# Experts in the order of their place in the group, result rows kept by expert number, and the final sums and norm beside the last experts

## The chip, the cores and the metric

The kernel runs on one core of one Trainium2 chip. The metric is the device time of one execution in microseconds, the median of three runs. The profiles come from single executions, recorded by the chip's profiler. TensorE multiplies matrices into PSUM, VectorE and ScalarE work on elements, GpSimd computes some elements and issues the indirect DMAs (gathers and scatters of rows by an index), and SyncE issues all other DMAs. Each engine, and each queue of DMA issues, executes its own list strictly in order.

## The reference

One layer of an encoder on 1024 tokens of width 1024 (batch 1, float32): a mixer of two attentions with a residual, a mixture of experts with a residual, and a last RMS norm. The mixer is not touched here. What matters:

```python
h = rms_norm(x, g_moe)
# 4 groups of 8 experts: the best group g_idx of each token, then the best 2 of its 8 experts
expert_ids = g_idx * 8 + idx                  # both experts of a token lie in one group
weights    = g_w * vals / sum(vals)
y_e        = (silu(h @ w1[e]) * (h @ w3[e])) @ w2[e]    # 1024 -> 512 -> 1024, 32 experts
x          = x + sum over the token's two experts of weight * y_e
out        = x * rsqrt(mean(x*x) + eps) * g_final
```

## The kernel before

**Stages.** Projections, attentions, the mixer's output with the routing of each tile of 128 tokens (`route_tile`), then the experts (`stage_moe`), then the final sums and norm. The values after the mixer (`x2`) and their norm (`h2`) are written to DRAM; the last four of the eight tiles of `x2` also stay in SBUF (`fx`).

**Routing and slots.** Each expert has 96 slots (`CAP`). A one-hot matmul over all tiles leaves in PSUM, for each expert and slot, the row of the result and the weight. `slots` makes from it three tiles with a column for each expert: `gi`, the token to gather; `yi`, the row of the result to write; `wt`, the weight. The result lies in a DRAM buffer `ys` of 2048 rows: row t for the token's best expert, row 1024 + t for its second. `ys` has been cleared to zeros before. Indices of empty slots are out of bounds, and the indirect DMA leaves them out. Tokens beyond the 96 go through `overflow`, a conditional part at the end that is skipped in these runs.

**One expert.** For expert e the weights w1, w3 and w2 come in six pieces of 1 MB (`expert_piece`, two for each matrix). Each is split into a rounded part (ScalarE, L45) and a remainder (VectorE, L46) in halves of 128x1024, and each product takes three matmuls (L1007 to L1009, L1039 to L1041). The 96 rows of `h2` are gathered (GpSimd) and transposed (TensorE); after w1 and w3 the gate's product (VectorE, L1018) waits for TensorE; the products are transposed and go through w2; ScalarE evicts with the weight, and GpSimd scatters the rows to `ys`. While expert e does this, w1 of expert e + 1 is multiplied, the rows of e + 2 are transposed and those of e + 3 gathered.

**Slots of the weights.** There are eleven buffers of 128x2048 (1 MB). `slot()` takes the first of a list and puts it back at its end, so the pieces go round; `slot(True)` takes one out of the round for good. A new tile in a buffer waits until all uses of the tile before it are done:

```python
    def slot(self, keep=False):
        p, i = self.free.pop(0)
        if not keep:
            self.free.append((p, i))
        return p.tile([128, 2 * D], F32, name=f"mraw{i}")
```

A piece is also issued only when the piece three before it has landed. All weight pieces, and the loads of the tail, stand in SyncE's one queue.

**Order.** TensorE's order is the written one (`manual_schedule`). For the other engines and queues a planner chooses: in its own model of the times it takes, whenever an engine is free, the ready instruction that is written first. The order is then fixed, and on the chip each instruction waits for its inputs in its place. `issue_after` adds an order between two instructions of one engine.

**The tail.** At expert 31 `final_rows` loads the gains and the four tiles of `x2` that are not in SBUF (L1192, L1198), and `final_sums` loads for each tile the rows of both halves of `ys` (L1208, 1 MB). GpSimd adds the first half (L1209). The rows of expert 31 are never written to `ys`: VectorE makes one-hot matrices of its tokens (L1107), and for each tile and 512 columns TensorE adds the second half (by an identity matmul, L1134) and expert 31's rows (two one-hot matmuls, L1135 and L1136), and VectorE adds that to the tile (L1137). The gains are broadcast by TensorE (L1184). `final_norm` takes squares and a square root on ScalarE (L1217, L1219), a reciprocal and the product on VectorE (L1220, L1221) and stores the tile (L1222).

## Time and profile before

| what | value |
|---|---|
| median of three runs | 1570.59 us (1570.49 to 1572.16) |
| the profiled execution | 1570.37 us, of which the profile's span is 1568.6 us |
| busy in the span | TensorE 95%, its weight loads 74%, VectorE 67%, ScalarE 56%, GpSimd 18% |
| chain that ended last | TensorE 81%, VectorE 6%, DMA 5%, ScalarE 2%, issue 3% |
| moved by DMA | 394.94 MB, 252 GB/s on the mean |

The experts run from about 906 us (first gather) to 1526 us, the tail from there to 1568.6. A timeline row gives start, length, engine (SPq is SyncE's DMA queue), line, operation, output<-input, shapes and count; in brackets stands how long the engine was idle before it and what released it. Several equal instructions in a row are merged, with their count behind an x and their common length. `mhi` and `mlo` are the rounded part and the remainder of a weight, `mraw` a buffer of the round, `m` and `mpy` PSUM tiles of the products, `mg` the gate's product.

### The profile page before, as it was taken

What the parts mean: (1) busy time and instruction counts of PE and PEld (TensorE: products, weight loads), DVE (VectorE), ACT (ScalarE), POOL (GpSimd) and SP (SyncE); (2) the same over time, 40 slices, a digit from 0 to 9 for tenths busy, and PEclk for the clock granted to TensorE, in tenths of its full rate; (3) what the DMA queues carried; (4) which work ended last, traced back from release to release, by engine and by line L of the source; (5) the groups of instructions that cost most, each with busy time, mean ns of one, the idle gap of its engine ahead of it and who ended that gap; (6) DMA issues with size and microseconds to landing.
All of it is one profiled execution on the core that took longest, in us unless ns stands there. A gap on an engine that the chain in (4) does not pass through costs nothing.

```text
span 1568.6 us, 21877 instructions
## 1 busy us (share of the span) xinstructions
PE 1483.5 (95%) x7713; PEld 1167.3 (74%) x7713; DVE 1050.8 (67%) x1926; ACT 881.6 (56%) x1328; POOL 289.4 (18%) x279
## 2 busy tenths in 40 slices
PE   7999999999999999989999869999999999999996
PEld 6998888788888888877888746666667666666663
DVE  6212566666655555628474579989998888888866
ACT  5312455455555555424121268878888777777763
POOL 2302122222212222200200211041001111111023
PEclk9999999999999999999999979999999999999998
DMA  8327888776545454389637579999999999999845
GB/s 268 123 95 211 232 239 239 222 219 181 160 136 174 135 155 128 106 252 284 228 122 288 207 242 372 368 359 370 381 380 378 366 350 346 353 347 350 316 173 216
DMA packets 179236, 394.94 MB, mean 252 GB/s; under 512 B 21714, under 2 KB 99538, under 8 KB 154546
## 3 DMA queue, kind: packets, MB, share of 16 engines
q1 hardware_dynamic: 172066, 376.89, 70.9%
q0 software_dynamic: 7056, 16.62, 3.3%
q8 instruction: 61, 1.00, 0.3%
q14 instruction: 53, 0.43, 0.1%
HBM read 324.36 MB, written 77.25 MB: 256 GB/s over the span
## 4 chain that ended last, share of the span: by engine, by line
PE 81%; DVE 6%; DMA 5%; issue 3%; ACT 2%; SPq 1%; POOL 0%; DVEq 0%; ACTq 0%; POOLq 0%
PE pz L308 7%; PE pz L310 7%; PE pz L309 7%; PE m L1008 6%; PE m L1009 6%; PE m L1007 6%; PE mpy L1041 3%; PE mpy L1039 3%; PE mpy L1040 3%; PE pt L389 3%; DMA mraw<-in_w_dram 3%; DVE mlo L46 3%; PE po L475 3%; PE ps L363 2%; PE ps L364 2%
## 5 line engine op out<-in xcount | busy, mean ns | idle before, releaser
L46 DVE TENSOR_TENSOR mlo<-mraw,mhi 128x1024 fp32r<-128x1024 f32 x384 | 450.1, 1220 | 41.3 <-ACT mhi L45 39.5
L45 ACT ACTIVATE mhi<-mraw 128x1024 fp32r<-128x1024 f32 x384 | 391.7, 1056 | 65.1 <-PE m L1009 47.7
L1008 PE MATMUL m<-mlo,XT 128*96 128x512 f32 x512 | 205.2, 401 | 22.4 <-DVE mlo L46 22.4
L308 PE MATMUL pz<-ht,zhi 128*128 128x512 f32 x512 | 214.1, 418 | 0.0
L1007 PE MATMUL m<-mhi,XT 128*96 128x512 f32 x512 | 206.2, 403 | 0.0
L1009 PE MATMUL m<-mhi,XT 128*96 128x512 f32 x512 | 204.8, 400 | 0.0
L310 PE MATMUL pz<-ht,zlo 128*128 128x512 f32 x512 | 201.4, 393 | 0.0
L309 PE MATMUL pz<-ht,zhi 128*128 128x512 f32 x512 | 200.1, 391 | 0.0
L372 ACT ACTIVATE te<-te,nm 128x256 f32<-128x256 f32 (+7 forms) x128 | 99.2, 775 | 118.0 <-DVE nm L368 117.7
L1008 PEld LDWEIGHTS m<-mlo,XT 128*96 128x96 f32 x512 | 84.2, 164 | 64.9 <-DVE mlo L46 31.1
L368 DVE CUSTOM_DVE_ANT_0 te<-ps,nF 128x512 f32<-128x512 f32 (+3 forms) x128 | 74.9, 587 | 61.3 <-PE ps L364 41.6
L310 PEld LDWEIGHTS pz<-ht,zlo 128*128 128x128 f32 x512 | 96.0, 188 | 21.6
L1009 PEld LDWEIGHTS m<-mhi,XT 128*96 128x96 f32 x512 | 83.9, 164 | 35.4 <-issue 0.8
L1007 PEld LDWEIGHTS m<-mhi,XT 128*96 128x96 f32 x512 | 84.0, 164 | 34.3 <-issue 0.5
L308 PEld LDWEIGHTS pz<-ht,zhi 128*128 128x128 f32 x512 | 97.5, 191 | 13.3
L309 PEld LDWEIGHTS pz<-ht,zhi 128*128 128x128 f32 x512 | 96.8, 189 | 13.3
L46 DVE TENSOR_TENSOR PT<-pt,PT 128x512 fp32r<-128x512 f32 (+1 forms) x144 | 76.7, 553 | 44.0 <-ACT PT L45 41.3
L1041 PE MATMUL mpy<-mhi,GT 128*96 128x512 f32 x256 | 101.7, 397 | 2.8 <-DVE GT L46 2.5
L1039 PE MATMUL mpy<-mhi,GT 128*96 128x512 f32 x256 | 102.3, 400 | 0.6 <-ACT GT L45 0.6
L280 POOL TENSOR_TENSOR zlo<-zraw,zhi 128x1024 fp32r<-128x1024 f32 x32 | 77.1, 2411 | 137.5 <-ACT zhi L279 123.4
L1040 PE MATMUL mpy<-mlo,GT 128*96 128x512 f32 x256 | 100.4, 392 | 0.0
L985 POOL DMA_INDIRECT X<-h,sg x32 | 39.2, 1226 | 327.3 <-PE mpt L995 320.3
(263 smaller groups left out, 2821.4 us busy)
## 6 DMA issues: line engine op xcount, KB each, us to landing
mraw<-in_w_dram SPq DMA_DIRECT2D x192, 1024.0 KB, 8.1
zraw<-in_w_in_dram SPq DMA_DIRECT2D x32, 512.0 KB, 4.9
ys<-ylast SPq DMA_DIRECT2D x16, 512.0 KB, 5.3
gscr<-sh SPq DMA_DIRECT2D x32, 256.0 KB, 2.1
o<-oscr SPq DMA_DIRECT2D x8, 1024.0 KB, 8.7
g<-gscr SPq DMA_DIRECT2D x32, 256.0 KB, 4.0
mraw<-ys SPq DMA_DIRECT2D x8, 1024.0 KB, 8.9
xt<-in_x_dram SPq DMA_DIRECT2D x8, 512.0 KB, 6.1
```

Of the source, the lines that this page charges most:

```text
L45: nc.scalar.activation(hi, src, AF.Copy)
L46: nc.vector.tensor_tensor(lo, src, f32(hi), op=OP.subtract)
L308: nc.tensor.matmul(ps, hi[:, k], self.hT[0][:, k, tk], start=(k == 0), stop=False)
L309: nc.tensor.matmul(ps, hi[:, k], self.hT[1][:, k, tk], start=False, stop=False)
L310: nc.tensor.matmul(ps, lo[:, k], self.hT[0][:, k, tk], start=False, stop=(k == KC - 1))
L372: nc.scalar.activation(t[:, :n], t[:, :n], AF.Exp, scale=-1.0, bias=nm, accum_out=rs)
L1007: nc.tensor.matmul(ps, XT[0][:, k], hi, start=(k == 0), stop=False)
L1008: nc.tensor.matmul(ps, XT[0][:, k], lo, start=False, stop=False)
L1009: nc.tensor.matmul(ps, XT[1][:, k], hi, start=False, stop=(k == KC - 1))
L1039: nc.tensor.matmul(ps[n], GT[0][:, k], hi[:, nn], start=(k == 0), stop=False)
L1040: nc.tensor.matmul(ps[n], GT[0][:, k], lo[:, nn], start=False, stop=False)
L1041: self.last_down = nc.tensor.matmul(ps[n], GT[1][:, k], hi[:, nn], start=False, stop=(k == 3))
```

## The change

- The experts are taken by `ORDER`: 0, 8, 16, 24, 1, 9, ..., 31, that is by their place in the group, and for equal places by group. Weights, `gi`, `yi` and `wt` are read by it.
- `route_tile` gives each token's two rows of `ys` by expert number: row t for the lower of its two experts, 1024 + t for the higher (three VectorE instructions more for each tile). So the first half of `ys` is complete when the first 28 experts in the new order are done, and a row of the last expert is always one of the second half.
- Before expert 28 is computed (that is, behind the weight loads of expert 29 in SyncE's queue): the gains (now broadcast by the DMA, 512 KB), the four tiles of `x2`, and the first half of `ys` in four loads of 1 MB through the round. VectorE adds it to the tiles at the end of experts 28 (tiles 0 to 3) and 29 (tiles 4 to 7).
- At expert 29: `x2` and the first half of `ys` are gathered for the last expert's tokens into a buffer of their own (`sl`) and added by VectorE. The down product of the last expert is evicted by VectorE with the weight, onto these rows.
- At the last expert: the second half of `ys`, four loads of 1 MB. VectorE adds it, then each tile is normed and stored. The square root is a power -0.5 on GpSimd (`rstd`).
- The rows of the last expert are normed apart and scattered to the output by token, over the rows that the tiles' stores have written there.
- The one-hot matrices, the sums on TensorE and GpSimd, the broadcast of the gains by TensorE and `tokf` go.

"Expert 28" here and below is the one at place 28 of the order, counted from 0.

```diff
+ORDER = [g * PER_GRP + l for l in range(PER_GRP) for g in range(N_GRP)]
...
-    def rstd(self, pool, ss, n, tag):
-        nc = self.nc
-        m = pool.tile([128, 1], F32, name=tag + "m")
+    def rstd(self, pool, ss, n, tag, q=128):
+        nc = self.nc
+        m = pool.tile([q, 1], F32, name=tag + "m")
         nc.vector.tensor_scalar(m, ss, 1.0 / n, EPS, op0=OP.mult, op1=OP.add)
-        r = pool.tile([128, 1], F32, name=tag + "r")
-        self.pow = nc.gpsimd.tensor_tensor(r, m, self.mhalf[:, 0:1], op=OP.pow)
+        r = pool.tile([q, 1], F32, name=tag + "r")
+        self.pow = nc.gpsimd.tensor_tensor(r, m, self.mhalf[:q, 0:1], op=OP.pow)
         return r
...
-        for k in range(2):
-            nc.vector.tensor_scalar(self.rec[:, :, k, 0], self.tok2[:, :, k], -PAD_ID, None, op0=OP.add)
+        nc.vector.tensor_scalar(self.tok2, self.tok2, -PAD_ID, None, op0=OP.add)
...
+        sw = p.tile([128, 1], F32, name="sw")
+        nc.vector.tensor_scalar(sw, ix[0], ix[1], float(S), op0=OP.is_lt, op1=OP.mult)
+        nc.vector.tensor_add(self.rec[:, t, 0, 0:1], self.tok2[:, t, 0:1], sw)
+        nc.vector.tensor_sub(self.rec[:, t, 1, 0:1], self.tok2[:, t, 1:2], sw)
...
-        nc.vector.tensor_copy(self.wt, tb[:, :, 1])
-        self.tokf = p.tile([CAP, 1], F32, name="stk")
-        self.slots_done = nc.vector.scalar_tensor_tensor(self.tokf, tb[:, N_EXP - 1, 0:1], PAD_ID, fi[:, N_EXP - 1:], op0=OP.add, op1=OP.add)
+        self.slots_done = nc.vector.tensor_copy(self.wt, tb[:, :, 1])
...
-        src = self.a[("w1", "w3", "w2")[wi]][0, e].rearrange("(p c) n -> p c n", p=128)
+        src = self.a[("w1", "w3", "w2")[wi]][0, ORDER[e] if isinstance(e, int) else e].rearrange("(p c) n -> p c n", p=128)
...
-            if hl:
-                split(nc, hl[0][:CAP, nn], hl[1][:CAP, nn], ps[n], wt)
-            nc.scalar.activation(y[:, nn], ps[n], AF.Copy, scale=wt)
+            if xs is not None:
+                nc.vector.scalar_tensor_tensor(xs[:, nn], ps[n], wt, xs[:, nn], op0=OP.mult, op1=OP.add)
+            else:
+                nc.scalar.activation(y[:, nn], ps[n], AF.Copy, scale=wt)
+        self.down_ps = ps
...
-        gi, yi = self.gi, self.yi
+        gi, yi, wt = [[x[:, o:o + 1] for o in ORDER] for x in (self.gi, self.yi, self.wt)]
...
-            if e == 31:
-                XS = self.final_rows(lambda: self.slot(True), self.fx)
...
-            else:
-                Y = self.final_sums(self.slot, XS, False)
-
-                oh = X[(e + 1) % XB].bitcast(F32R)
-                for t in range(NT):
-                    nc.vector.tensor_scalar(oh[:, t * 128:(t + 1) * 128], self.jcol[:CAP], self.tokf, float(-t * 128),
-                                            op0=OP.subtract, op1=OP.is_equal)
+
+            if e == N_EXP - 4:
+                XS = self.final_rows(lambda: self.slot(True), self.fx)
+                Y = self.final_load(self.slot, 0)
+            if e == N_EXP - 3:
+
+                sl = self.slot(True)[:CAP]
+                for half, src in ((0, self.x2), (1, self.ys)):
+                    nc.gpsimd.indirect_dma_start(out=sl[:, half * D:(half + 1) * D], out_offset=None, in_=src,
+                                                 in_offset=bass.IndirectOffsetOnAxis(ap=gi[-1], axis=0),
+                                                 bounds_check=S - 1, oob_is_err=False)
+                nc.vector.tensor_add(sl[:, :D], sl[:, :D], sl[:, D:])
+            if last:
+                Y = self.final_load(self.slot, 1)
...
-                    self.expert_gather(X[(e + 1) % XB], gi[:, e + 3:e + 4])
-            hl = [X[e % XB].bitcast(F32R), self.wh.tile([128, D], F32R, name="mlo")[:CAP]] if last else None
-            y = self.expert_down(GT, w, self.wt[:, e:e + 1], self.ylast if last else None, hl)
+                    self.expert_gather(X[(e + 1) % XB], gi[e + 3])
+            y = self.expert_down(GT, w, wt[e], sl if last else None)
             if not last:
-                self.scatter_y(y, yi[:, e:e + 1])
+                self.scatter_y(y, yi[e])
+            if N_EXP - 4 <= e < N_EXP - 2:
+                for t in range(NT)[e % 2 * 4:e % 2 * 4 + 4]:
+                    nc.vector.tensor_add(XS[t], XS[t], Y[t])
...
-        with self.tc.issue_after(self.last_down.ins):
-            self.final_gains(self.pab)
-
+
+        self.fp = p
+        junk = self.slot(True)
         for t in range(NT):
-            for n in range(2):
-                nn = slice(n * 512, (n + 1) * 512)
-                ps = self.pab.tile([128, 512], F32, name=f"m{n}", bufs=2 - n)
-                with self.tc.issue_after(self.last_down.ins):
-                    nc.tensor.matmul(ps, self.ident, Y[t][:, 1, nn], start=True, stop=False)
-                nc.tensor.matmul(ps, oh[:, t * 128:(t + 1) * 128], hl[0][:, nn], start=False, stop=False)
-                nc.tensor.matmul(ps, oh[:, t * 128:(t + 1) * 128], hl[1][:, nn], start=False, stop=True)
-                nc.vector.tensor_add(XS[t][:, nn], ps, XS[t][:, nn])
-            self.final_norm(t, XS[t], Y[t].rearrange("p k d -> p (k d)"))
+            nc.vector.tensor_add(XS[t], XS[t], Y[t])
+            self.final_norm(t, XS[t], junk[:, t % 2 * D:(t % 2 + 1) * D], Y[t])
...
+        ss = p.tile([CAP, 1], F32, name="ssl")
+        nc.scalar.activation(sl[:, D:], sl[:, :D], AF.Square, accum_out=ss)
+        r = self.rstd(p, ss, D, "rl", CAP)
+        nc.vector.scalar_tensor_tensor(sl[:, D:], sl[:, :D], r, self.gfin[:CAP], op0=OP.mult, op1=OP.mult)
+        nc.gpsimd.indirect_dma_start(out=a["out"][0], out_offset=bass.IndirectOffsetOnAxis(ap=gi[-1], axis=0),
+                                     in_=sl[:, D:], in_offset=None, bounds_check=S - 1, oob_is_err=False)
+        for n in range(2):
+            nc.scalar.activation(self.ylast[:, n * 512:(n + 1) * 512], self.down_ps[n], AF.Copy, scale=wt[-1])
...
-        g = self.gfin = tile()
-        nc.sync.dma_start(g[0:1, D:], self.a["g_final"].rearrange("(o d) -> o d", o=1))
+        self.gfin = tile()[:, :D]
+        nc.sync.dma_start(self.gfin, self.bcast(self.a["g_final"]))
...
-    def final_sums(self, tile, X, both):
-
-        nc = self.nc
-        Y = []
-        for t in range(NT):
-            y = tile().rearrange("p (k d) -> p k d", k=2)
-            Y.append(y)
-            nc.sync.dma_start(y, self.ys.rearrange("(k t) d -> t k d", k=2)[t * 128:(t + 1) * 128])
-            nc.gpsimd.tensor_tensor(X[t], X[t], y[:, 0], op=OP.add)
-            if both:
-                nc.vector.tensor_add(X[t], X[t], y[:, 1])
+    def final_load(self, tile, k):
+
+        Y = {}
+        for t in range(0, NT, 2):
+            y = tile()
+            self.nc.sync.dma_start(y.rearrange("p (t d) -> p t d", t=2),
+                                   self.ys[k * S + t * 128:k * S + (t + 2) * 128].rearrange("(t p) d -> p t d", p=128))
+            for i in range(2):
+                Y[t + i] = y[:, i * D:(i + 1) * D]
         return Y
 
-    def final_norm(self, t, x, y):
-        nc = self.nc
-        ss = self.rp.tile([128, 1], F32, name="ssf", bufs=2)
-        nc.scalar.activation(y[:, :D], x, AF.Square, accum_out=ss)
-        r = self.rp.tile([128, 1], F32, name="rfr", bufs=2)
-        nc.scalar.activation(r, ss, AF.Sqrt, scale=1.0 / D, bias=self.eps)
-        nc.vector.reciprocal(r, r)
-        nc.vector.scalar_tensor_tensor(y[:, D:], x, r, self.gfin[:, :D], op0=OP.mult, op1=OP.mult)
-        nc.sync.dma_start(self.a["out"][0, t * 128:(t + 1) * 128], y[:, D:])
+    def final_norm(self, t, x, junk, y):
+
+        nc = self.nc
+        ss = self.fp.tile([128, 1], F32, name=f"ssf{t % 2}")
+        nc.scalar.activation(junk, x, AF.Square, accum_out=ss)
+        r = self.rstd(self.fp, ss, D, f"rf{t % 2}")
+        nc.vector.scalar_tensor_tensor(y, x, r, self.gfin, op0=OP.mult, op1=OP.mult)
+        self.nc.sync.dma_start(self.a["out"][0, t * 128:(t + 1) * 128], y)
```

## Rows read from the trace of the kernel before

**Rows 1.** By window: length, engines' busy us (instructions), clock, DMA share, GB/s

```profile
1440.00:1460.00 20.00, 18.09 (x79) 12.78 (x80) 16.56 (x17) 13.77 (x18) 2.31 (x2) 0.91 0.88 314
1460.00:1480.00 20.00, 19.27 (x90) 13.14 (x88) 17.92 (x25) 16.40 (x21) 1.45 (x1) 1.00 0.96 348
1480.00:1500.00 20.00, 18.00 (x86) 12.83 (x87) 17.70 (x18) 15.19 (x19) 1.04 (x1) 1.00 0.70 262
1500.00:1520.00 20.00, 17.61 (x80) 11.87 (x79) 15.41 (x15) 11.70 (x14) 1.20 (x1) 1.00 0.10 29
...
1526.00:1540.00 14.00, 12.77 (x32) 6.31 (x30) 8.23 (x11) 6.76 (x12) 12.95 (x6) 0.88 1.02 406
```

**Rows 2.** Timeline of SyncE's DMA queue: start, length, line, transfer, count

```profile
1438.17 45.27 SPq L964 DMA_DIRECT2D mraw<-in_w_dram  x14
...
1517.61 6.72 SPq L1208 DMA_DIRECT2D mraw<-ys  x8
```

**Rows 3.** Timeline of TensorE: the last matmul of expert 31

```profile
1525.36 0.40 PE L1041 MATMUL mpy<-mhi,GT 128*96 128x512 f32 x1
```

**Rows 4.** Timeline of GpSimd, the tail; in brackets its idle time and releaser

```profile
1522.64 4.83 POOL L1209 TENSOR_TENSOR mraw<-mraw,mraw 128x1024 f32<-128x1024 f32 x2 [7.57 <-DMA mraw<-ys]
1527.68 2.35 POOL L1209 TENSOR_TENSOR mraw<-mraw,mraw 128x1024 f32<-128x1024 f32 x1 [0.21 <-DMA mraw<-ys]
...
1537.97 6.39 POOL L1209 TENSOR_TENSOR fx<-fx,mraw 128x1024 f32<-128x1024 f32 x2 [0.18 <-DMA mraw<-ys]
```

**Rows 5.** Timeline of VectorE, end of expert 31 and tail

```profile
1508.57 3.50 DVE L46 TENSOR_TENSOR mlo<-mraw,mhi 128x1024 fp32r<-128x1024 f32 x3 [0.70 <-ACT mhi L45]
...
1525.81 1.44 DVE L49 SCALAR_TENSOR_TENSOR mlo<-mpy,sw,X 96x512 fp32r<-96x512 f32 x2 [5.42 <-ACT X L48]
...
1535.96 2.91 DVE L1221 SCALAR_TENSOR_TENSOR mraw<-mraw,rfr,mraw 128x1024 f32<-128x1024 f32 x1
...
1561.25 1.29 DVE L1221 SCALAR_TENSOR_TENSOR mraw<-fx,rfr,mraw 128x1024 f32<-128x1024 f32 x1
```

**Rows 6.** Timeline of VectorE: an instruction of one column, at the slots

```profile
905.43 0.14 DVE L874 SCALAR_TENSOR_TENSOR stk<-ptb,sf 96x1 f32<-96x1 f32 x1
```

**Rows 7.** DMA issues after 1505: queue, operation, count, KB each, us to landing

```profile
out_dram<-mraw SPq DMA_DIRECT2D x8, 512.0 KB, 2.6
ys<-my,sy POOLq DMA_INDIRECT x1, 3.7
```

**Rows 8.** Timeline of VectorE: a normalization in the first stage

```profile
32.73 1.28 DVE L170 SCALAR_TENSOR_TENSOR h<-xt,r1r,gm 128x1024 f32<-128x1024 f32 x1 [0.73 <-POOL r1r L127]
```

**Rows 9.** Groups by line, experts' stage: busy us, mean ns of one

```profile
L1107 DVE TENSOR_SCALAR X<-jcol,stk 96x128 fp32r<-96x128 f32 x8 | 1.8, 288 | 0.0
```

**Rows 10.** Timeline of VectorE, experts 27 to 30: products (L1018) and remainders (L46)

```profile
1439.68 1.04 DVE L1018 TENSOR_TENSOR mg<-m,mg 96x512 f32<-96x512 f32 x1 [1.54 <-PE m L1009]
...
1461.18 1.10 DVE L1018 TENSOR_TENSOR mg<-m,mg 96x512 f32<-96x512 f32 x1 [0.41 <-PE m L1009]
...
1479.77 1.04 DVE L1018 TENSOR_TENSOR mg<-m,mg 96x512 f32<-96x512 f32 x1 [0.50 <-PE m L1009]
1480.72 5.76 DVE L46 TENSOR_TENSOR mlo<-mraw,mhi 128x1024 fp32r<-128x1024 f32 x5
...
1499.72 1.10 DVE L1018 TENSOR_TENSOR mg<-m,mg 96x512 f32<-96x512 f32 x1 [0.40 <-PE m L1009]
```

**Rows 11.** Timeline of GpSimd: the scatter of expert 27's rows

```profile
1456.57 1.06 POOL L1050 DMA_INDIRECT ys<-my,sy  x1 [5.03 <-ACT my L1046]
```

**Rows 12.** DMA issues: all scatters of rows; weight loads between 1460 and 1480

```profile
ys<-my,sy POOLq DMA_INDIRECT x31, 7.8
...
mraw<-in_w_dram SPq DMA_DIRECT2D x6, 1024.0 KB, 7.1
```

**Rows 13.** Timeline of VectorE: the products of experts 7 and 14

```profile
1065.25 1.07 DVE L1018 TENSOR_TENSOR mg<-m,mg 96x512 f32<-96x512 f32 x1
...
1190.77 1.08 DVE L1018 TENSOR_TENSOR mg<-m,mg 96x512 f32<-96x512 f32 x1
```

More of the change, by code (lines that the diff above doesn't have):

```diff
@@ L72, in constants @@
         nc.vector.tensor_scalar(self.ident, jp, 0.0, None, op0=OP.is_equal)
-        self.eps = c.tile([128, 1], F32, name="eps")
-        nc.vector.memset(self.eps, EPS)
         self.mhalf = c.tile([128, 8], F32, name="mhalf")
@@ L1028, in expert_g, with expert_down @@
         return GT
-    def expert_down(self, GT, w, wt, y=None, hl=None):
+    def expert_down(self, GT, w, wt, xs=None):
         nc = self.nc
-        if y is None:
-            y = self.xp.tile([CAP, D], F32, name="my", bufs=1)
+        y = None if xs is not None else self.xp.tile([CAP, D], F32, name="my", bufs=1)
         ps = [self.py.tile([CAP, 512], F32, name="mpy") for _ in range(2)]
@@ L1040, in expert_down @@
                 nc.tensor.matmul(ps[n], GT[0][:, k], lo[:, nn], start=False, stop=False)
-                self.last_down = nc.tensor.matmul(ps[n], GT[1][:, k], hi[:, nn], start=False, stop=(k == 3))
+                nc.tensor.matmul(ps[n], GT[1][:, k], hi[:, nn], start=False, stop=(k == 3))
         for n in range(2):
             nn = slice(n * 512, (n + 1) * 512)
-            if hl:
-                split(nc, hl[0][:CAP, nn], hl[1][:CAP, nn], ps[n], wt)
-            nc.scalar.activation(y[:, nn], ps[n], AF.Copy, scale=wt)
+            if xs is not None:
[3 more added lines that the diff above has]
+        self.down_ps = ps
         return y
@@ L1089, in stage_moe @@
         for e in range(2):
-            self.expert_gather(X[e], gi[:, e:e + 1])
+            self.expert_gather(X[e], gi[e])
         XT = {e: self.expert_x(X[e]) for e in range(2)}
-        self.expert_gather(X[0], gi[:, 2:3])
+        self.expert_gather(X[0], gi[2])
         up0 = self.expert_up(XT[0], weights(0, [0]))
@@ L1139, in stage_moe @@
         self.yilast = self.rp.tile([CAP, 1], I32, name="yilast")
-        nc.vector.tensor_copy(self.yilast, yi[:, N_EXP - 1:])
+        nc.vector.tensor_copy(self.yilast, yi[-1])
     def overflow(self):
@@ L1173, in overflow @@
                 X = self.final_rows(y, {})
-                self.final_gains(self.pool(st, "opg", space=PSUM))
-                self.final_sums(y, X, True)
+                self.fp = p
+                for k in range(2):
+                    for t, r in self.final_load(y, k).items():
+                        nc.vector.tensor_add(X[t], X[t], r)
                 for t in range(NT):
-                    self.final_norm(t, X[t], y())
-    def final_gains(self, psum):
-        g = self.gfin
-        for n in range(2):
-            ps = psum.tile([128, 512], F32, name=f"m{n}", bufs=2 - n)
-            self.nc.tensor.matmul(ps, self.ones1[0:1, 0:1].to_broadcast([1, 128]), g[0:1, D + n * 512:D + (n + 1) * 512],
-                                  start=True, stop=True)
-            self.nc.scalar.activation(g[:, n * 512:(n + 1) * 512], ps, AF.Copy)
+                    o = y()
+                    self.final_norm(t, X[t], o[:, :D], o[:, D:])
     def final_rows(self, tile, X):
         nc = self.nc
-        g = self.gfin = tile()
-        nc.sync.dma_start(g[0:1, D:], self.a["g_final"].rearrange("(o d) -> o d", o=1))
+        self.gfin = tile()[:, :D]
+        nc.sync.dma_start(self.gfin, self.bcast(self.a["g_final"]))
         ts = [t for t in range(NT) if t not in X]
@@ L1199, in final_rows @@
         return X
-    def final_sums(self, tile, X, both):
-        nc = self.nc
-        Y = []
-        for t in range(NT):
-            y = tile().rearrange("p (k d) -> p k d", k=2)
-            Y.append(y)
-            nc.sync.dma_start(y, self.ys.rearrange("(k t) d -> t k d", k=2)[t * 128:(t + 1) * 128])
-            nc.gpsimd.tensor_tensor(X[t], X[t], y[:, 0], op=OP.add)
-            if both:
-                nc.vector.tensor_add(X[t], X[t], y[:, 1])
-        return Y
-    def final_norm(self, t, x, y):
-        nc = self.nc
-        ss = self.rp.tile([128, 1], F32, name="ssf", bufs=2)
-        nc.scalar.activation(y[:, :D], x, AF.Square, accum_out=ss)
-        r = self.rp.tile([128, 1], F32, name="rfr", bufs=2)
-        nc.scalar.activation(r, ss, AF.Sqrt, scale=1.0 / D, bias=self.eps)
-        nc.vector.reciprocal(r, r)
-        nc.vector.scalar_tensor_tensor(y[:, D:], x, r, self.gfin[:, :D], op0=OP.mult, op1=OP.mult)
-        nc.sync.dma_start(self.a["out"][0, t * 128:(t + 1) * 128], y[:, D:])
+    def final_load(self, tile, k):
[6 more added lines that the diff above has]
+                Y[t + i] = y[:, i * D:(i + 1) * D]
+        return Y
+    def final_norm(self, t, x, junk, y):
+        nc = self.nc
+        ss = self.fp.tile([128, 1], F32, name=f"ssf{t % 2}")
[3 more added lines that the diff above has]
+        self.nc.sync.dma_start(self.a["out"][0, t * 128:(t + 1) * 128], y)
     def run(self):
```

## The prediction

> **What bounds the kernel now.** I read the table by windows first. In the last experts TensorE is the busiest engine, VectorE is close behind it (17.92 and 17.70 of 20 us), and the DMA engines are at 0.96 of their time until 1480, then 0.70, then 0.10: the last weights are issued by 1483.4 and the DMAs stand nearly idle while experts 30 and 31 are computed [rows 1, 2]. From the start of expert 31's last matmul, 1525.36, it is another 43.2 us to the end of the span, 1568.6 [rows 3]. In these, first a transfer sets the pace: eight loads of `ys`, 1 MB each, can start only at 1517.61, when expert 30's rows have been scattered, and run at 406 GB/s. GpSimd adds them as they land, from 1522.64, one every 2.57 us [rows 1, 2, 4]. Then VectorE paces: its normalization takes 1.29 us alone but 2.91 us beside a GpSimd addition, and the last one starts at 1561.25 [rows 5]. So the change has these 43 us to work on, and it pays with work that it puts among experts 28 to 31.
>
> **The tail, part by part.** All times are on the clock of the profile before; a delay d from the experts shifts them and is sized below.
> 1. Only the second half of `ys` is still to be loaded at the end: 4 MB in four loads instead of 8 MB. They still wait for the scatter of expert 30 (the wait stays, half the bytes go). The first lands at 1522.64 as now, the fourth three intervals of 2.57 us later, 1530.4 [rows 4].
> 2. The sums move from GpSimd and from TensorE (identity and one-hot matmuls, gains broadcast by matmul) to VectorE. Per tile: one sum of 128x1024 (1.17 us: three two-input instructions of that size in a row take 3.50 [rows 5]), an instruction on one column (0.14 [rows 6]), the normalization without a GpSimd sum beside it (1.29): 2.60, eight tiles 20.8. Expert 31's own 96 rows: two evictions of 512 columns (1.44 together [rows 5]), 0.14 and 1.29, so 2.9. Together 23.7 us, from 1522.64 to 1546.3. The loads (done 1530.4) and the squares on ScalarE run beneath it; TensorE's share of the tail, and a Sqrt with its reciprocal, go. I cost them at nothing because VectorE is late next in any case.
> 3. The last tile's store lands 2.6 us after its issue, with 0.1 to start it: 1549.0. New: expert 31's rows are scattered over the same output, so the scatter waits for all eight stores. It is the last on GpSimd's queue and nothing stands behind it. Issue to landing of a scatter with the DMAs idle is 3.7 us, and the stores' 2.6 us stand in the same view [rows 7]: 1552.7. The present end lies 3.4 us behind the landing of the last store (issue 1562.6, landing 1565.2, end 1568.6); the same again gives 1556.1.
> So the tail alone is worth 1568.6 - 1556.1 = 12.5 us.
>
> On the power by GpSimd that replaces the Sqrt: before each normalization in the first stage VectorE stood idle 0.73 us for it at most, although VectorE's own two-input instructions ran around it [rows 8]. The Trainium skill (SBUF — State Buffer, "Who interferes with whom") says that a VectorE instruction with two SBUF inputs and a GpSimd instruction that reads SBUF exclude each other for a whole instruction. The trace agrees for long ones (2.91 against 1.29 us [rows 5]); by the rule each power could also wait out a sum, 1.17 us for each of eight tiles or 9.4 us, and the sum below would come to 1573.9, which the wait in rows 8 doesn't bear out. I put the powers beneath the next tile's sum, at nothing, and make their exposure a rival.
>
> **What the experts pay (d).**
> 1. VectorE gets eight sums for the first half, due in experts 28 and 29 (8 x 1.17 = 9.3), and one sum of 96 rows (1.1); the eight one-hot instructions go (1.8 [rows 9]). Net 8.6 us. Between 1460 and 1520 it is idle 60 - 51.0 = 9.0 us [rows 1]. Not all of that can be used, since it works in a fixed order: it waits for TensorE before the gate's product. The 1.8 us of one-hots lay in such gaps: the wait before the product is 0.50 us at 1479.77 against 1.54 us two experts earlier, and that expert took 18.59 us, less than the 19.95 of the next [rows 10]. Bounds: 0 (all in gaps) to 8.6 (none). I take half the idle time as usable: 4.3.
> 2. SP's queue. The four loads of the first half stand ahead of expert 30's six weight loads and wait until expert 27's rows are scattered: issued 1456.57, landing 7.8 us later, 1464.4 [rows 11, 12]. Four MB at 406 GB/s, 10.3 us: 1474.7. Expert 30's first piece would land about 2.6 to 7.1 us behind that, at 1477.3 to 1481.8, and its first remainder is computed at 1480.72 now, some 2.3 us after it must be there (ScalarE's copy and the remainder, each counted as one sum) [rows 10, 12]. Bounds: 0 to 3.4; I take 2. The later pieces (three of eleven slots kept, four more lent until the sums are done) each have an expert more time; the x2 rows and the gains go out before the wait, and the idle DMAs of 1500 to 1520 take up the displaced weights.
> 3. A stall can halve TensorE's clock for a while: the expert from 1439.68 to 1461.18 took 21.50 us with a granted clock of 0.91 in that window, against 19.95 at 1.00 [rows 1, 10]. Bounds 0 to 1.6 for one such dip more or fewer; I take 0, since d is late work that TensorE waits for either way.
> 4. Before the experts: three 128x1 instructions more per tile in the routing, hidden beside matmuls for seven tiles, on the path for the last; one less at the slots. At 0.14 us each, net two: 0.3; bounds 0 to 0.5. The new order of the experts changes which columns of the index tiles are read, and costs nothing: each expert still takes 96 slots.
> The two gathers of x2 and `ys` rows for expert 31 go on GpSimd's queue ahead of the scatter of expert 29 and cost GpSimd about 1.1 us each; behind them only scatters wait. I put them at nothing; if VectorE's sum of these rows is queued too early it stalls, within the upper bound of 1.
> So d = 4.3 + 2 + 0.3 = 6.6, between 0 and 8.6 + 3.4 + 1.6 + 0.5 = 14.1.
>
> **Sum.** 1556.1 + 6.6 = 1562.7 for the span. The profiled execution took 1570.37 for a span of 1568.6, so 1.8 us lie around it: 1564.5 us. The median of the runs is 0.2 us above the profiled execution, which I neglect. Forecast: 1564.5, 6 us or 0.4% faster. Its own range is 1560.5 to 1567.4.
>
> **Rivals.**
> - *All of it hidden.* The sums fall into VectorE's gaps as the one-hots did, and expert 30's weights come in time: d about 0.5, 1558.4. For it: the 9 us of idle VectorE and the idle DMAs of 1500 to 1520. Against: TensorE already waits for VectorE's remainders inside most late experts (the mean from 1190.77 to 1499.72 is 308.95/16 = 19.3 us an expert, from 1065.25 to 1190.77 it was 17.93 [rows 10, 13]). Chance 0.18.
> - *The power is exposed.* If VectorE's order puts each normalization right behind its own power, it waits 0.73 us nine times, 6.6 us: 1571.1, no change. (By the Trainium skill's rule above the wait would be longer.) For it: that wait in the first stage. Against: there are always other tiles' sums to do until the last two tiles. Chance 0.11.
> - *Slower: expert 31's weights wait for the sums.* Two of the slots that the first half borrows go next to expert 31's first piece and to the tile of its tokens. That piece can be issued only when the sums of tiles 6 and 7 are done, and SP's queue stands behind it. If these come only with the end of expert 29's work on VectorE, near 1499.72, the piece lands 7.1 us later and is ready after 2.3 more, 9.4 us after TensorE wants it. With the full 8.6 of the sums, 3.4 of expert 30 and the 0.5 of the routing, d is 21.9: 1556.1 + 21.9 + 1.8 = 1579.8. It decides when d goes beyond 15.8 (1573.7). For it: one queue, in order, and no other lead than the slots. Against: the one-hots, written behind expert 30, were executed between 1460 and 1480, beside experts 28 and 29 (VectorE's 25 instructions there, 17 and 18 in the windows around it [rows 1]), so ready work is drawn forward. Chance 0.14.
> - *The order of VectorE changes wholesale.* Experts 7 to 14 take 17.93 us each, 28 to 30 in the mean (18.59 + 19.95)/2 = 19.27 with the same instructions: early, no product waits for TensorE [rows 13], late, each does [rows 10], and the remainders stand behind it. If the change moves the point where the planner's order turns from one to the other by five experts, that is 5 x 1.34 = 6.7 us, and a clock dip of 1.55 with it, either way: 1556.3 or 1572.7. Chance 0.07, half each way.
> Forecast: 0.50.
>
> **How the numbers follow.** Without a change, repeated runs agree to about 0.2%, 3.1 us: faster is below 1567.5, slower above 1573.7. Faster: the forecast but for its upper edge (0.47), all hidden (0.18), half the wholesale case (0.03): 0.68. Same: 0.03 of the forecast, 0.10 of the exposed power, 0.02 of the slower case, 0.02 of the wholesale case: 0.17. Slower: 0.12 of the slower case, 0.01 of the exposed power and 0.02 of the wholesale case: 0.15. The range holds the forecast, the hidden case with the shift downward, the exposed power and the slower case's mild end: 1553 to 1575.
>
> **What would show it.** In the changed profile: four loads of `ys` of 1 MB that land about 10 us after the last scatter of rows; VectorE busy nearly without a gap for some 23 us from there; no TensorE work after expert 31; a scatter to the output issued about 2.7 us after the last store and landing 3.7 later. From the last down matmul to the end of the span: 31 us instead of 43. Starts of the gate's product in experts 28 to 31 give d: 6 us later than now at expert 31. VectorE idle for GpSimd's power in the tail would show the second rival, SP waiting on VectorE's sums at expert 31's weights the third, other starts of the product before expert 27 the fourth. I'm wrong if the last down matmul is later by over 10 us, or the tail longer than 34.

## The result: 1592.3 us, 1.3% slower

The changed kernel takes 1592.32 us (median of 4 runs, 1591.66 to 1595.56) beside 1570.54 (1569.73 to 1572.16) for the kernel before in the same session: ratio 1.0133, 95% interval 1.0118 to 1.0147. The forecast was 1564.5 us, in a range of 1553 to 1575. The profiled execution has a span of 1589.9 us, 21.3 longer than before.

**How to split the 21.3.** Each expert has one gate product on VectorE, so its starts are a ruler. Line numbers have moved: the product is L1020 (before L1018), remainders and other splits L48 (L46), sums of the first half L1134, the sum of the last expert's rows L1115, sums of the second half L1141, normalization L1225 (L1221). Times in us, worked out from the products' starts in the VectorE timelines and the spans:

| | product of expert 0 to 29 | 29 to 30 | 30 to 31 | 31 to end of span |
|---|---|---|---|---|
| before | 546.57 | 19.95 | 17.93 | 50.95 |
| changed | 546.24 | 42.40 | 17.95 | 47.9 |

Expert 29 alone grows by 22.45 us; the tail gives back 3.05 instead of 12.5. The product of expert 0 starts 2.23 us later (935.43 against 933.20): the routing takes 1.7 more (shown below), it starts 1.3 later, and the stretch between it and expert 0 is 0.7 shorter. The start of the routing differs by more than that between traces of one and the same routing (751.83 in d1, 756.51 in g1, both below), so the 1.3 is not put down to the change. The sum is 2.23 - 0.33 + 22.45 + 0.02 - 3.05 = 21.3.

**Expert 29.** The timeline of VectorE after the change, from the product of expert 29 (start, length, engine, line, operation, tiles, count; in brackets the idle time before it and what ended it). It answers to [rows 10].

```profile
1481.67 1.05 DVE L1020 TENSOR_TENSOR mg<-m,mg 96x512 f32<-96x512 f32 x1 [1.53 <-PE m L1011]
1482.62 4.62 DVE L1134 TENSOR_TENSOR mraw<-mraw,mraw 128x1024 f32<-128x1024 f32 x4
1487.17 4.62 DVE L1134 TENSOR_TENSOR fx<-fx,mraw 128x1024 f32<-128x1024 f32 x4
1491.71 3.48 DVE L48 TENSOR_TENSOR mlo<-mraw,mhi 128x1024 fp32r<-128x1024 f32 x3
1506.87 1.22 DVE L1115 TENSOR_TENSOR mraw<-mraw 96x1024 f32<-96x1024 f32 x1 [11.68 <-DMA mraw<-ys,sg]
1508.01 2.35 DVE L48 TENSOR_TENSOR mlo<-mraw,mhi 128x1024 fp32r<-128x1024 f32 x2
...
1524.07 1.10 DVE L1020 TENSOR_TENSOR mg<-m,mg 96x512 f32<-96x512 f32 x1 [0.40 <-PE m L1011]
```

Right behind the product, where five remainders stood before, all eight sums run, and later the sum of the last expert's rows holds the queue for 11.68 us, since a gather has not landed. TensorE's timeline in the same stretch shows who pays, both times waiting for a remainder of VectorE:

```profile
1492.98 0.74 PE L1010 MATMUL m<-mlo,XT 128*96 128x512 f32 x1 [11.11 <-DVE mlo L48]
1509.28 0.74 PE L1010 MATMUL m<-mlo,XT 128*96 128x512 f32 x1 [8.80 <-DVE mlo L48]
```

Why the gather was late stands in GpSimd's timeline:

```profile
1490.27 5.76 POOL L1112 DMA_INDIRECT mraw<-x,sg  x1 [30.73 <-DMA mraw<-in_w_dram]
1496.34 0.95 POOL L1054 DMA_INDIRECT ys<-my,sy  x1 [0.30 <-issue]
1503.05 0.97 POOL L1112 DMA_INDIRECT mraw<-ys,sg  x1 [5.76 <-DMA ys<-my,sy]
```

The gather of `x2` rows needs a slot that the first half's sums of tiles 4 and 5 give back, and starts 0.8 us after them (the profile puts its wait down to a weight load; without the sums, in d1 below, it starts at 1472). Behind it in the queue stand the scatter of expert 28 and the gather of `ys` rows, which waits for that scatter to land. The first gather is also slow in itself: 5.76 us on GpSimd against 1.68 in d1, while VectorE runs without a gap until 1495.19. The kernel before has the same at expert 4, where VectorE is busy for all of 1020 to 1030 and a scatter takes 12.55 us, most others about 1:

```profile
1020.40 12.55 POOL L1050 DMA_INDIRECT ys<-my,sy  x1 [6.90 <-ACT my L1046]
```

That VectorE's work draws out GpSimd's DMA instruction fits both rows, but no run separates it.

The windows show the clock, in answer to [rows 1] (length, busy us and instructions of PE, PEld, DVE, ACT, POOL, clock, DMA share, GB/s):

```profile
1480.00:1490.00 10.00, 1.87 (x9) 0.98 (x7) 8.47 (x9) 3.42 (x4) 0.00 (x0) 0.77 0.89 339
1490.00:1500.00 10.00, 7.02 (x21) 4.72 (x22) 5.19 (x5) 2.11 (x2) 6.71 (x2) 0.55 0.83 303
1500.00:1510.00 10.00, 1.20 (x6) 0.73 (x5) 3.13 (x3) 0.49 (x1) 0.97 (x1) 0.62 0.13 42
```

Beside and after TensorE's standstills the clock is granted at 0.77, 0.55 and 0.62 in the mean, so for most of the last two windows at the lower of its two levels (1.2 of 2.4 GHz). The two waits are 19.9 us; expert 29 lost 22.45, which leaves about 2.5; the lower clock fits them, but nothing separates it.

**The tail.** Last down matmul (answers to [rows 3]), first sum of the second half, a normalization that waits for its power, the last one:

```profile
1549.74 0.40 PE L1043 MATMUL mpy<-mhi,GT 128*96 128x512 f32 x1
```

```profile
1546.85 2.36 DVE L1141 TENSOR_TENSOR mraw<-mraw,mraw 128x1024 f32<-128x1024 f32 x2 [2.09 <-DMA mraw<-ys]
...
1556.77 1.28 DVE L1225 SCALAR_TENSOR_TENSOR mraw<-mraw,rf0r,mraw 128x1024 f32<-128x1024 f32 x1 [0.45 <-POOL rf0r L127]
...
1571.13 1.27 DVE L1225 SCALAR_TENSOR_TENSOR mraw<-fx,rf1r,mraw 128x1024 f32<-128x1024 f32 x1
```

GpSimd in the tail: a power issued while a VectorE sum runs, one issued while VectorE is idle (its next instruction starts 0.06 us later), the scatter of the last rows; then two instructions of its queue at the end, from the views of their lines (durations in ns, least/median/most, first and last start):

```profile
1555.34 1.40 POOL L127 TENSOR_TENSOR rf0r<-rf0m,mhalf 128x1 f32<-128x1 f32 x1 [2.19 <-DVE rf0m L125]
...
1569.87 0.55 POOL L127 TENSOR_TENSOR rf1r<-rf1m,mhalf 128x1 f32<-128x1 f32 x1
1578.63 0.95 POOL L1148 DMA_INDIRECT out_dram<-mraw,sg  x1 [8.21 <-issue]
```

```profile
L1159 POOLq INC_SWDGE_SEM  x1: 1496/1496/1496, 1582.1 to 1582.1; - x1
```

```profile
L1290 POOLq DRAIN  x3: 46/107/5458, 1583.6 to 1589.6; - x3
```

The scatter lands 3.4 us after its issue, about 1582.0. Then GpSimd counts up a semaphore for 1.5 us, drains for 5.46, and the span ends. The kernel before has the same two instructions, but they start at 1544.8, under VectorE's work, and cost nothing:

```profile
L1286 POOLq DRAIN  x3: 46/107/5213, 1546.3 to 1568.3; - x3
```

### The profile page after: what moved, and what is told of

It reads as the page before. It is cut to its first block, busy times and chain, and to the rows that moved or that the text cites. A ratio compares the mean times of both kernels' runs of the same rounds, so it can differ in the third digit from the quotient of the medians.

```text
span 1589.9 us, 21741 instructions
## 1 busy us (share of the span) xinstructions
PE 1461.7 (92%) x7645; PEld 1156.5 (73%) x7645; DVE 1057.1 (66%) x1942; ACT 878.4 (55%) x1317; POOL 285.5 (18%) x283
## 5 line engine op out<-in xcount | busy, mean ns | idle before, releaser
L48 DVE TENSOR_TENSOR mlo<-mraw,mhi 128x1024 fp32r<-128x1024 f32 x384 | 449.9, 1219 | 41.4 <-ACT mhi L47 39.7
L48 DVE TENSOR_TENSOR PT<-pt,PT 128x512 fp32r<-128x512 f32 (+1 forms) x144 | 76.6, 552 | 43.3 <-ACT PT L47 40.6
```

What stands on the lines that cost most here:

```text
L48: nc.vector.tensor_tensor(lo, src, f32(hi), op=OP.subtract)
```

## The experiments

Theory: VectorE's fixed order puts work that TensorE does not need ahead of remainders that it needs, and a GpSimd transfer as the last act lays GpSimd's own end bare. Rival: the slots kept and lent and SP's queue starve the last weights. Times are medians, and each ratio is to the kernel before on the same chip, whose medians lie between 1572.2 and 1572.6. The last four columns come from one profiled execution each. In these an expert from 16 to 27 takes 18.6 us and 19.9 or 21.5 in turn, in every kernel but v1, so 1.5 us more or less in a column can be one such expert (the 21.52 of b2 is).

| kernel | time, us | ratio (95%) | 0 to 29 | 29 to 30 | 30 to 31 | 31 to end |
|---|---|---|---|---|---|---|
| a1_sum_last | 1581.54 | 1.0055 (1.0039, 1.0072) | 544.66 | 31.32 | 17.93 | 47.9 |
| a2_sums_split | 1584.86 | 1.0083 (1.0064, 1.0103) | 546.66 | 34.16 | 23.14 | 45.5 |
| a3_both | 1577.76 | 1.0035 (1.0020, 1.0049) | 549.54 | 24.04 | 22.50 | 47.0 |
| d1_no_sums | 1571.35 | 0.9997 (0.9984, 1.0009) | 546.89 | 19.92 | 17.95 | 49.9 |
| c1_no_scatter | 1581.93 | 1.0062 (1.0044, 1.0080) | 547.23 | 42.45 | 17.95 | 36.6 |
| b1_exit_gpsimd | 1578.37 | 1.0034 (1.0019, 1.0049) | 546.76 | 19.95 | 17.92 | 56.1 |
| b2_row_rule | 1574.86 | 1.0011 (0.9996, 1.0025) | 546.78 | 21.52 | 17.94 | 50.8 |
| h1_sums_gpsimd | 1583.58 | 1.0068 (1.0048, 1.0088) | 555.09 | 27.38 | 17.95 | 46.3 |
| v1_order_before | 1570.52 | 0.9987 (0.9974, 1.0000) | 545.82 | 19.32 | 20.92 | 51.4 |
| g1_merge_tail | 1573.20 | 0.9998 (0.9982, 1.0013) | 549.66 | 22.84 | 22.07 | 37.8 |
| g2_sums_in_gaps | 1573.84 | 1.0007 (0.9995, 1.0020) | 546.54 | 25.54 | 17.91 | 43.4 |
| g3_loads_earlier | 1569.37 | 0.9978 (0.9967, 0.9990) | 546.32 | 25.68 | 17.88 | 39.5 |

**a1: the last expert's sum behind the last product.**

```diff
-                nc.vector.tensor_add(sl[:, :D], sl[:, :D], sl[:, D:])
...
+            if last:
+                with self.tc.issue_after(self.last_mul.ins):
+                    nc.vector.tensor_add(sl[:, :D], sl[:, :D], sl[:, D:])
```

> The changed kernel with one move: VectorE adds the gathered rows of the last expert behind that expert's gate product instead of ahead of two remainders in expert 29. Theory (VectorE's fixed order puts work that TensorE does not need ahead of remainders that it needs): TensorE's 8.80 us wait of expert 29 goes, the gap from product 29 to product 30 falls from 42.4 us to about 33, and the whole by 8 to 10 us, to about 1583. Rival (lent weight slots and SP's queue starve the weights): nothing changes, 1592.

One instruction of 1.2 us, moved, is worth 11 us: expert 29 falls from 42.40 to 31.32, more than the wait of 8.80, since TensorE is at full clock again sooner (1.00 from 1500 to 1510, where the changed kernel had 0.62). TensorE's waits between 1470 and 1560 (us, times, longest) keep the first stall:

```profile
PE m L1010 <- DVE mlo L48: 11.8, 2, 11.1
```

**a2: the eight sums in two batches; a3: both moves.**

```diff
+                with self.tc.issue_after(self.xt_done.ins):
+                    for t in range(NT)[e % 2 * 4:e % 2 * 4 + 4]:
+                        self.summed = nc.vector.tensor_add(XS[t], XS[t], Y[t])
...
+            with self.tc.issue_after((self.summed if near else self.slots_done).ins):
+                g = self.expert_gated(up0, up1)
...
+                w0 = weights(e + 1, [0])
+                w = weights(e, [2]) if near else w
```

> The changed kernel with the eight sums of the first half's rows taken apart: four behind the split of XT for expert 30 and four behind the split of XT for expert 31, and the splits of w2 in these two experts put behind those of the next expert's w1. The last expert's sum stays where the change has it. Theory: TensorE's 11.11 us wait in expert 29 goes; the second batch of sums costs expert 30 some 5 us; the whole falls by 5 to 9 us, to about 1585. Rival of the weights: nothing changes, 1592.

> Both moves of the two kernels before it together. Theory: expert 29 runs at its old length and expert 30 pays about 5 us, so the whole falls by 13 to 18 us, to about 1577, still above the 1570.5 of the kernel before since the tail and routing keep their cost. Rival of the weights: 1592.

Both came out as the theory had it. In a2 no wait of TensorE is longer than 7.7 us, and the 11.1 us stall is gone; VectorE stands at the last expert's sum again:

```profile
1507.03 1.22 DVE L1115 TENSOR_TENSOR mraw<-mraw 96x1024 f32<-96x1024 f32 x1 [6.95 <-DMA mraw<-ys,sg]
```

In a3 no wait of TensorE in this stretch is longer than 2.0 us. Expert 29 still pays 4.1 us and expert 30 4.6, 8.7 for sums of 9.2. (The 3.0 us ahead of product 29 are not theirs: they lie in experts 5, 6 and 17.) So the stalls are gone, but the placing is not yet good, and here late weights have a part. ScalarE, which reads each weight first, waits for weights 8.0 us between 1478 and 1545 (total, times, longest), where it waited 1.2 in the changed kernel, and TensorE waits 3.0 us for ScalarE. Whether the slots lent to the sums or those of w2, now split later, hold the weights up is not shown:

```profile
ACT mhi L47 <- DMA mraw<-in_w_dram: 8.0, 3, 4.5
```

**d1: a1 without the eight sums, their loads kept.**

```diff
-                for t in range(NT)[e % 2 * 4:e % 2 * 4 + 4]:
-                    nc.vector.tensor_add(XS[t], XS[t], Y[t])
```

> The changed kernel with the last expert's sum moved behind its product, and without the eight sums of the first half (the first of each token's two expert rows is left out of the output; its loads stay). Theory: with the sums gone, expert 29 has its old length, the gap from product 29 to product 30 falls from 31.3 us to about 20, and the whole by 11 us against the kernel that only moves the last expert's sum, from 1581.5 to about 1570.5. Rival (the loads of the first half and the queue of SP delay the weights): the gap stays above 30 us and the time above 1580.

The gap is 19.92 us against 19.95 before the change. The first half's loads stay at their old place in SP's queue, and the last experts lose nothing to them, so the queue is out as the cause. The lent slots are not tested by d1: without the sums they come back as soon as their loads have landed. For these the trace of the changed kernel speaks. SP's queue does wait 9.1 us for the sums there, and the last weight is issued at 1519.15 (before: 1483.1), but ScalarE waits for weights only 1.2 us in all between 1478 and 1545:

```profile
ACT mhi L47 <- DMA mraw<-in_w_dram: 1.2, 2, 0.7
```

So the rival does not carry the 22 us. The gather, too, starts 18 us earlier in d1 than in the changed kernel:

```profile
1472.13 1.68 POOL L1112 DMA_INDIRECT mraw<-x,sg  x1 [14.65 <-DVE mlo L48]
```

**c1: no last scatter; b1: the kernel before with GpSimd's transfer as its last act.**

```diff
 c1
-        nc.gpsimd.indirect_dma_start(out=a["out"][0], out_offset=bass.IndirectOffsetOnAxis(ap=gi[-1], axis=0),
-                                     in_=sl[:, D:], in_offset=None, bounds_check=S - 1, oob_is_err=False)
 b1
-        nc.sync.dma_start(self.a["out"][0, t * 128:(t + 1) * 128], y[:, D:])
+        (nc.gpsimd if t == NT - 1 else nc.sync).dma_start(self.a["out"][0, t * 128:(t + 1) * 128], y[:, D:])
```

> The changed kernel without the last scatter: the rows of the last expert's tokens are not written. Theory (with GpSimd's DMA as the last act, GpSimd's end, 1.5 us of a semaphore and 5.5 us of a drain, stands bare behind the landing): the end falls by the scatter's own way, about 6.5 us from 1575.5 to 1582.0, and by the bare end, about 4.5 us more, so by 10 to 11 us to about 1581.5. Rival (the end costs the same behind any engine's last transfer): 6 to 6.5 us, to about 1586.

> The kernel before, with one edit: the store of the last tile of the output is issued by GpSimd instead of SP. Theory (a program whose last transfer is GpSimd's ends about 7.9 us behind its landing, against 3.4 us behind one of SP's, since GpSimd's semaphore of 1.5 us and its drain of some 5.4 us can start only then): 4 to 7 us slower than the kernel before, about 1576. Rival (the end of the changed kernel is long for another reason, such as the indirect form of its scatter): no change, 1570.5.

The scatter costs 47.9 - 36.6 = 11.3 us of tail. Even without it GpSimd ends last: its drain runs from 1572.8 to 1578.2, since its last power comes only at 1570.2, while SP's own drains are ready at 1576.8, so some 1.3 us of GpSimd's end stay bare in c1.

```profile
L1288 POOLq DRAIN  x3: 46/107/5377, 1572.8 to 1578.7; - x3
L1288 SPq DRAIN  x3: 7/7/13, 1576.8 to 1578.4; - x3
```

An ordinary store does the same to the kernel before: from the end of the last normalization to the end of the span it was 6.1 us (1562.54 to 1568.6) and is 11.4 in b1 (1564.51 to 1575.9), with the drain now at the very end:

```profile
1564.82 0.62 POOL L1222 DMA_DIRECT2D out_dram<-mraw  x1 [18.34 <-DVEq L1146]
```

```profile
L1286 POOLq DRAIN  x3: 46/113/5295, 1569.7 to 1575.6; - x3
```

**b2: the rule of the rows alone.**

```diff
+        sw = p.tile([128, 1], F32, name="sw")
+        nc.vector.tensor_scalar(sw, ix[0], ix[1], float(S), op0=OP.is_lt, op1=OP.mult)
+        nc.vector.tensor_add(self.rec[:, t, 0, 0:1], self.tok2[:, t, 0:1], sw)
+        nc.vector.tensor_sub(self.rec[:, t, 1, 0:1], self.tok2[:, t, 1:2], sw)
```

> The kernel before, with one part of the change: the row of an assignment goes by the expert number, which is three more VectorE instructions for each of the eight tiles in the routing. Experts run in the old order and the end is the old one. Theory (nothing hides them, as the tiles of the changed kernel came 0.2 us apart more than before): 1.5 to 2.5 us slower. The forecast's own step: 0.3 us.

By the whole time it can't be told from nothing; by the tiles it can. GpSimd's power in the first and the last tile of the routing, before and in b2:

```profile
753.39 0.56 POOL L127 TENSOR_TENSOR r2r<-r2m,mhalf 128x1 f32<-128x1 f32 x1 [72.56 <-DVE r2m L125]
...
897.00 0.55 POOL L127 TENSOR_TENSOR r2r<-r2m,mhalf 128x1 f32<-128x1 f32 x1 [2.49 <-DVE r2m L125]
```

```profile
756.48 0.56 POOL L129 TENSOR_TENSOR r2r<-r2m,mhalf 128x1 f32<-128x1 f32 x1 [72.81 <-DVE r2m L127]
...
901.71 0.55 POOL L129 TENSOR_TENSOR r2r<-r2m,mhalf 128x1 f32<-128x1 f32 x1 [2.38 <-DVE r2m L127]
```

Seven intervals take 143.61 us before and 145.23 in b2 (145.29 in the changed kernel, 143.60 in b1, which lacks the rule): 1.6 to 1.7 us, 0.24 a tile.

**h1: a1 with the sums on GpSimd.**

```diff
-                    nc.vector.tensor_add(XS[t], XS[t], Y[t])
+                    nc.gpsimd.tensor_tensor(XS[t], XS[t], Y[t], op=OP.add)
```

> The kernel that only moves the last expert's sum (1581.5), with the eight sums of the first half on GpSimd, which has little else to do in the experts. Theory (VectorE's remainders and GpSimd's sums, both reading two arrays of SBUF, keep each other out, as the norm's power of 0.55 us took 1.4 us beside a sum): nothing is won against VectorE's sums, since a sum takes GpSimd 2.4 us where it takes VectorE 1.16: 1580 to 1592. Rival (the two engines work side by side): the sums vanish as in the kernel without them, 1571.

No gain. VectorE's remainders, 1.16 us in a row elsewhere, take 16.92/6 = 2.82 beside GpSimd's sums, and these take 12.47/4 = 3.12 instead of 2.35:

```profile
1473.12 16.92 DVE L48 TENSOR_TENSOR mlo<-mraw,mhi 128x1024 fp32r<-128x1024 f32 x6
```

```profile
1468.78 12.47 POOL L1136 TENSOR_TENSOR mraw<-mraw,mraw 128x1024 f32<-128x1024 f32 x4 [9.03 <-DVE mlo L48]
```

**v1: the kernel before with each w2 behind the next w1.**

```diff
-            w = weights(e, [2])
...
+                w0 = weights(e + 1, [0])
+                w = weights(e, [2])
```

> The kernel before, with one edit: the splits of each expert's w2 are put behind those of the next expert's w1, the order in which TensorE consumes them. Theory of the fixed order: in the later experts TensorE waits 16 times for a remainder, 19 us in all, because VectorE is then at one that TensorE needs later; a part of these waits goes, and the time falls by 5 to 19 us. Rival (the weights' DMA, at 0.95 to 1.00 of its engines, sets the pace): no change, 1570 to 1573.

Inconclusive. TensorE's 16 waits for a remainder between 1000 and 1480 became 19 waits for the split of GT, now behind w2's (26.3 us instead of 19.0), so the order was changed without being improved.

**g1 to g3: towards a version that keeps the gain.** g1 is a3 with the old merge of the last expert (one-hots, TensorE, a Sqrt) in place of gathers and scatter; of the second half's sums VectorE keeps two tiles, in g2 and g3 one. g2 puts four sums behind product 29 and the split of XT for expert 31, and four behind the last product. g3 frees the loads of the last four tiles from a scatter that they need not wait for.

```diff
 g2
+                    for t in range(e % 2 * 2, e % 2 * 2 + 2):
+                        nc.vector.tensor_add(XS[t], XS[t], YA[t])
...
+                for t in range(4, NT):
+                    with self.tc.issue_after(self.last_mul.ins):
+                        nc.vector.tensor_add(XS[t], XS[t], YA[t])
 g3
+            if e == N_EXP - 2:
+                YA.update(self.final_load(self.slot, 0, range(4, NT, 2)))
             if last:
-                YA.update(self.final_load(self.slot, 0, range(4, NT, 2)))
                 Y = self.final_load(self.slot, 1)
```

> The version with both moves of the sums (1577.8), and the old way of bringing in the last expert: one-hot matmuls of TensorE add its rows to each tile, ScalarE and VectorE make the norm's factor, and there are no gathers and no last scatter. Theory: VectorE needs about 2.7 us for a tile, so product 31 to the end is 8 us of expert 31, 3 us of splits, 23 us of tiles and 6 us of the last store, some 40 us instead of 47: about 1571, level with the kernel before. If the end behind a GpSimd scatter costs nothing of its own, it stays at 1577.

> The version with the old merge of the last expert, with the sums of the first half put where VectorE waits: two behind product 29, two behind the split of XT for expert 31, and four, with the one-hots, behind the last product, where VectorE was idle for some 5 us; the loads of these last four come after the last weights. Theory (an instruction of VectorE costs the experts its length wherever TensorE waits for what stands behind it, and nothing in the idle of expert 31): from the first product to the last 594.6 us become 586 to 589, and the end stays some 38.5 us behind it: about 1562 to 1565, faster than the kernel before. Rival (sums cost the same wherever they stand): about 1573.

> The version before it with one edit: the loads of the last four first-half tiles are written into the program ahead of the scatter of expert 30, so they need not wait for it. They were issued 1524.96, with the last product, and landed some 5 us later, so that two sums stood ahead of the second split of the last expert's rows and TensorE began the merge 3 us late. Theory: the four sums are done before the last down projection ends, product 31 to the end falls from 43.4 us to 38 to 39.5, and the whole by 4 to 5 us: some 1566 to 1569, faster than the kernel before by 3 to 6. Rival (these loads now take the place of the last weights, or TensorE's merge sets the end): 1572 to 1574.

g1 came out 2 us above its 1571, level with the kernel before as forecast. Its tail is 37.8 us, 13.2 shorter than before: about what was forecast for the tail, without a transfer by GpSimd at its end. g2 missed. From the first to the last product it is 4.6 us shorter (594.57 to 589.99), but 3.1 of that lie ahead of product 29; experts 29 and 30 got back only 1.5, since the four sums that stay there still cost 5.6 us in expert 29 (25.54 against 19.95). And the tail grew by 5.6, because the late loads set the sums between the two splits of the last expert's rows. g3 mended that: VectorE behind its last product,

```profile
1528.59 4.62 DVE L1128 TENSOR_TENSOR fx<-fx,mraw 128x1024 f32<-128x1024 f32 x4
1533.71 1.44 DVE L51 SCALAR_TENSOR_TENSOR mlo<-mpy,sw,X 96x512 fp32r<-96x512 f32 x2 [0.51 <-ACT X L50]
```

four sums in what had been idle time (5.42 us in [rows 5]): from the last product to the first of these splits it is 8.17 us, before the change 8.16. g3 beats both kernels: 0.22% (0.10 to 0.33) below the kernel before, 3 us.

## Why the prediction was wrong

- **Step 1 of the experts' delay is the step that failed.** It took the sums for work of 8.6 us, half hidden (4.3), with 8.6 as the most. Measured: 22.45 us in expert 29. Two things were left out. Idle time of VectorE is of no use to a sum that stands ahead of a remainder that TensorE is about to need, and all eight stood there: 11.4 us of gap (a1 against d1). And an instruction that waits costs its wait, not its length: the 96-row sum "within the upper bound" cost 11.1 (a1). The row that should have warned is [rows 10]: right behind the product of 1479.77, five remainders at once. And the 18.59 against 19.95 us that it took for a trace of the one-hots is the rhythm of the late experts in the traces without one-hots too.
- **The gathers at nothing.** The text named what is queued behind them (scatters) but not what is queued behind the sum that awaits them, nor that their slot comes from the sums.
- **Step 2, SP's queue (2 us, 0 to 3.4)**: 0 in d1. The first-half loads went out 4.4 us behind the scatter they wait for (1458.46 to 1462.85), where the text took 7.8.
- **Step 3, the clock (0, up to 1.6)**: about 2.5 us, what expert 29 lost beyond its two waits; 2.3 of it are the part of a1's gain that is not its wait.
- **Step 4, the routing (0.3, at most 0.5)**: 1.6 to 1.7. Each of the seven intervals between tiles grew, so no tile hid the three instructions.
- **The tail (12.5 us).** From the last down matmul to the end it is 40.2 us instead of 30.7. The loads were right: the first sum starts 2.9 us ahead of that matmul, forecast 2.7. VectorE took 25.55 us instead of 23.7, with 2.85 of idle time for powers costed at nothing. Step 3 failed: the scatter starts some 3 us behind the landing of the last store, not at once, and the end comes 7.9 us behind its landing, not "the same again" 3.4. Of the 9.4 us lost, 1.7 are VectorE's, 3.2 the late start, 4.5 the end; b1 shows the last by itself. Of the 8.21 us of "issue" before the scatter, GpSimd waits for the stores until 1576.0; the other 2.6 are not a fixed price. They are 2.6 to 3.3 us in the changed kernel, a1 and d1, where one packet of the DMA's instruction queue (q14 in the profile) falls into them, and 0.8 in a2, a3 and h1, where none does. That GpSimd waits for instructions there is not shown by any run.
- **The rivals.** Hidden: refuted by the stall. Exposed power: 2.85 of its 6.6 us came. Here the row and the rule of the Trainium skill (SBUF — State Buffer, "Who interferes with whom") come together: a power issued beside a running sum takes 1.39 to 1.55 us, one issued in VectorE's idle time 0.55; h1 shows the same from the other side, 16.92 us for six remainders of 1.16, which leaves 9.9 us, about four GpSimd sums of 2.35 [rows 4]. Where the power comes first the trace does not bear the rule out: the one at 1569.87 runs for 0.5 us beside a normalization, and neither is longer than elsewhere (0.55 and 1.28 us). The 9.4 us worked out by the rule was too much, since the wait hides under the sum itself: VectorE lost only what was left of a power behind it, 0.44 to 0.60 us six times. Slower: right in sign, wrong in mechanism; SP did wait for VectorE's sums, as its sign said, but TensorE waited for VectorE, never for expert 31's weights. Wholesale order: refuted, 546.24 against 546.57 us for 29 experts.

Both signs of being wrong that the prediction named came: the last down matmul is 24.4 us later (over 10), and the tail is 40.2 us (over 34).

Not settled: what the "issue" time ahead of the last scatter is. The 2 us by which d1's tail is longer than that of a1 lie at two places: 1.6 between the last product and the last down matmul (9.29 against 7.72 us, at a granted clock of 0.78 against 1.00), 0.5 behind the last normalization.

## What to carry to other kernels

Price work that is moved onto a busy engine by what stands behind it in that engine's order, and an instruction that waits by its wait: idle share is no room. Put such work where the engine's next consumer is late anyway (behind the last product, 4.6 us of sums cost nothing), and trace its input's whole chain, slot and queue included. When a change makes another engine's transfer the last act, that engine's own end has to be read from a trace, not taken over from the engine that ended before.

## Not expected of the hardware

- GpSimd's end: 1.44 to 1.50 us for a semaphore and a drain of 5.21 to 5.46 us in the traces of before, changed, c1 and b1, hidden only in before; with GpSimd's transfer last, the span ends 5.3 us later behind the last normalization (b1).
- VectorE and GpSimd adding arrays side by side take about the sum of their times (h1), so GpSimd was no spare adder beside these remainders.
